# Moving key searches, context work and modulation rows inside a fused PEER and scan kernel

## The chip, the core and the metric

The kernel runs on one core of a Trainium2 chip. The metric is the device time of one launch in microseconds, the median of several executions. The engines are named as in the profile: PE (TensorE, matrix products), DVE (VectorE), ACT (ScalarE), POOL (GpSimd) and SP (SyncE, which only issues transfers here). Each engine, and the list of transfers of SP and of POOL, executes its own program strictly in order.

## What is computed

Two transformer-like blocks on 256 tokens of width 1024, in float32. The first block is a normalisation, one wide projection, an attention that selects keys by an index score, a convolution branch, and then PEER: each token picks 16 of 16384 experts in each of 8 heads and gathers their rows. The second block normalises with shifts and scales that come from `c` (the modulation rows), runs a context of 256 other tokens through a gated linear recurrence (RWKV) in both directions, runs the tokens through the same recurrence from the states so won, and ends with a convolutional feed-forward part.

```python
def peer(h, w_query, sub_keys, expert_u, expert_v):
    q = (h @ w_query).reshape(B, S, 8, 2, 128)
    sc = einsum("bshcd,hckd->bshck", q, sub_keys)   # key scores: 2 x 128 per head and token
    sv, si = top_k(sc, 16)                          # the search
    cand_s = sv[..., 0, :, None] + sv[..., 1, None, :]
    top_s, top_j = top_k(cand_s, 16); eidx = ...    # 16 experts of 16384
    gate = softmax(top_s)
    u = expert_u[eidx]; v = expert_v[eidx]          # gathered rows, 1024 each
    return sum(gelu(u . h) * gate * v)

mod = silu(c) @ ada_w + ada_b                       # modulation rows, for the tokens
cmod = silu(c_ctx) @ ada_w + ada_b                  # and for the context
```

## The kernel before

Line numbers are those of the profile of the kernel before; where the changed kernel's order is shown, they are 3 higher for the searches, the attention and the experts, and 16 to 19 higher from line 950 on.

The 256 tokens are two tiles of 128. The program is written in Python over a framework that gives every instruction a priority by the place where the code issues it, plays the program through a model of the engines, and from that fixes one order for each engine; `tc.issue_after(i)` keeps what stands under it behind instruction `i`. So the order in which code is written sets who goes first, and after that the chip only waits, it does not reorder.

- **0 to 291 us.** The first block up to its residual: index scores (`index(t)`, L629, products L637), gated linear units, queries, keys, values, gates, attention (`attention(t)`, L664: logits L675 and L676, softmax on DVE and ACT, transposes L691, value products L695), the convolution (L762, mean L767), and six modulation rows. A modulation row (`ada_row`, L391) loads 2 MB, multiplies it on DVE by columns of `silu(c)` (L407, 7 instructions of 128x512 for each of its one or two vectors), and has PE sum over the partitions (L412). Rows 0 to 3 are made for the tokens and for the context (n = 2), rows 4 and 5 for the tokens alone; all six are written behind the convolution.
- **291 to 1160 us.** The experts: 16 units, a unit being one head of one tile, first the 8 of tile 0. A unit (`experts`, L865) gathers 16 times 1 MB with an indirect transfer (L875, 9 buffers `G`), forms each gather's scalar products with the tokens on DVE (L880, the dots), and for groups of four the gelu (L886 to L892) and the sum with V, even members on PE (L903, L905) and odd ones on DVE (L909). At the end of a tile the PE sum is added (L896).
- Before a head's unit its keys must be known: `subkeys(h)` (L458) makes the query and the scores of both tiles on PE, `best(t, h, sc)` (L476) searches 16 of 128 twice on DVE (L483 to L487), and `pairs`, `route` and `weigh` pick the 16 experts. `AHEAD` makes heads 1 to 7 within units 1 to 4 of tile 0, and there each head's `best` runs for tile 0 and, behind the unit, also for tile 1. For tile 1 only `pairs`, `route` and `weigh` are left, three units ahead (`LEAD`).
- In the same stretch the engines do other work between the dots: the context's part (its scans, L1006 to L1260), `front(0)` (the second block's first products on tile 0) and `scans0` (the local part of tile 0's scans, both directions d = 0, 1, at the end of which d = 1's MN, RQ and Y are stored). In the code they stand behind all 16 units, so they have the lower priority, and fill what the units leave.
- **1160 to 1591 us.** `front(1)` (from L322), the scans of tile 1 and their combination with tile 0's, modulation rows 6 to 11, the output product and the feed-forward part. SP's loads for it begin with `yy<-Y` (L1526: tile 0's scan outputs, into the buffer that `h` of tile 1 leaves) and the weights.

PSUM banks are handed out by `bank(tag)`: `"ac0"` and `"ac1"` name one bank each, `"ac"` takes them in turn.

Of the kernel before, what the change touches and what calls it, by code (L numbers as in the profile page):

```python
# [25 lines left out]
F32 = mybir.dt.float32  # L26
# [3 lines left out]
AF = mybir.ActivationFunctionType  # L30
# [62 lines left out]
def block_kernel(ctx: ExitStack, tc: tile.TileContext, I, out):  # L93
# [363 lines left out]

    def subkeys(h):  # L458
# [8 lines left out]
        sc = {t: pa.tile([128, 256], F32, tag="sc", name="sc", bufs=6) for t in range(NT)}  # L467
        for t in range(NT):
# [4 lines left out]
            nc.scalar.activation(sc[t], p[:, :256], AF.Copy)  # L473
        return sc
# [71 lines left out]
    with ExitStack() as st:  # L546
# [82 lines left out]
        def index(t):  # L629
# [3 lines left out]
            for g in range(2):  # L633
                for s in range(2):
                    p = bank("ac0")
# [28 lines left out]
        def attention(t):  # L664
# [4 lines left out]
            for g in range(2):  # L669
                for s in range(2):  # L670
                    p = bank("ac0")
# [15 lines left out]
            po = bank("ac0")  # L687
# [24 lines left out]
        for t in range(NT):  # L712
            index(t)

# [13 lines left out]
        sc2 = scv.rearrange("p k s -> p (k s)")  # L728
        nc.scalar.activation(sc2, V("c"), AF.Sigmoid)
        nc.vector.tensor_tensor(sc2, sc2, V("c"), op=OP.mult)  # L730
# [12 lines left out]
        pada = pool("pada", stack=st)  # L743
# [20 lines left out]
        run(chain(*[ada_row(pada, j, 2) for j in range(4)]))  # L764
# [21 lines left out]
        run(chain(*[ada_row(pada, j, 1) for j in range(4, 6)]))  # L786
# [130 lines left out]
    for t in range(NT):  # L917
        if t == 1:
            h2[1] = ph.tile([128, D], F32, tag="h2", name="h2")
            nc.sync.dma_start(out=h2[1], in_=h2d)  # L920
        pacc = [bank("ac", 2) for _ in range(2)]
        for h in range(H):
            if t == 0:
                for g in AHEAD.get(h, ()):
                    with after(*ends, first_gather[0]):
                        sc[g] = subkeys(g)
                    best(0, g, sc[g][0])
                    weigh(0, g, *route(0, g, *pairs(0, g, nc.gpsimd)))
            else:
                for g in range(h + 1 if h else 0, min(h + 2, H)):  # L930
                    with tc.issue_after(unit_end[H + g - LEAD]):
                        weigh(1, g, *route(1, g, *pairs(1, g, nc.gpsimd)))
            unit_end.append(experts(t, h, pacc))
            if t == 0:
                if h == 0:
                    sc01 = pe.tile([128, 256], F32, tag="sc0", name="sc01")
                    subkeys_one(1, sc01)
                    best(1, 0, sc01)
                for g in AHEAD.get(h, ()):
                    best(1, g, sc[g][1])  # L940
# [884 lines left out]
```

## Time and profile before

| | us |
|---|---|
| median of three runs | 1593.75 (1590.28 to 1598.25) |
| the profiled execution | 1593.02 |
| its span in the trace | 1591.3 |
| first gather issued | 291.3 |
| last dots end | 1158.2 |
| VectorE busy in all | 1139.2 |

The trace shows one execution. A row of a group of instructions names the engine, the line, the tile written, the tiles read and a shape; "idle before" is time in which the engine had nothing to do ahead of these instructions, with what ended it. Of TensorE's clock 1.00 is 2.4 GHz and 0.50 is 1.2 GHz.

### The profile page before, as it was taken

How to read it: one execution, taken by the hardware profiler on the slowest of the kernel's cores; microseconds unless marked ns; L12 is line 12 of the kernel's file. 1: busy time of each engine (PE TensorE's matmuls, PEld its weight loads, DVE VectorE, ACT ScalarE, POOL GpSimd, SP SyncE). 2: the span in 40 equal slices, each digit the busy share in tenths (PEclk: the TensorE clock that was granted, in tenths of full speed). 3: DMA queues.
4: the chain of work that ended last, by engine and by line, in shares of the span. 5: the costliest groups of instructions: out<-in, count | busy, mean ns of one | idle time of the engine just before them, and what ended most of it. 6: DMA issues, size and time to landing. Idle time of an engine off the chain costs nothing. (4 is left out here: it accounts for less than half of the span.)

```text
span 1591.3 us, 26450 instructions
## 1 busy us (share of the span) xinstructions
PE 1363.7 (86%) x10140; PEld 889.3 (56%) x10140; DVE 1139.2 (72%) x2495; ACT 516.4 (32%) x1290; POOL 600.4 (38%) x599
## 2 busy tenths in 40 slices
PE   7999979888878888887884979988679898599997
PEld 5744554666435554545432335645344577399997
DVE  3991573699969888989665687787842966456676
ACT  3122230332243333333233242233232223244543
POOL 0000001245555655565542564254500211356663
PEclk9999959999988888878897989879889889799999
DMA  9545463698898999896997999979987541446561
GB/s 352 187 146 167 137 213 111 254 351 329 322 388 304 392 370 368 329 351 266 416 416 308 398 402 357 362 276 380 408 315 274 178 142 57 170 132 188 181 189 53
DMA packets 90197, 435.12 MB, mean 273 GB/s; under 512 B 9996, under 2 KB 14620, under 8 KB 57304
## 3 DMA queue, kind: packets, MB, share of 16 engines
q0 software_dynamic: 36864, 268.45, 42.8%
q1 hardware_dynamic: 52488, 163.67, 30.0%
q8 instruction: 80, 1.31, 0.3%
q10 hardware_dynamic: 720, 1.31, 0.2%
q14 instruction: 45, 0.37, 0.1%
HBM read 428.39 MB, written 5.01 MB: 272 GB/s over the span
## 5 line engine op out<-in xcount | busy, mean ns | idle before, releaser
L875 POOL DMA_INDIRECT G<-in_experts,eidx x256 | 335.2, 1309 | 356.9 <-DVE x L909 229.3
L880 DVE SCALAR_TENSOR_TENSOR G<-G,h 128x1024 f32<-128x1024 f32 x256 | 322.7, 1272 | 18.4 <-DMA G<-in_experts,eidx 14.9
L905 PE MATMUL ac<-G,dg 128*128 128x512 f32 x504 | 280.3, 705 | 51.4 <-ACT dg L903 51.1
L905 PEld LDWEIGHTS ac<-G,dg 128*128 128x128 f32 x504 | 108.6, 226 | 189.1 <-issue 115.0
L909 DVE SCALAR_TENSOR_TENSOR x<-G,ga,x 128x1024 f32<-128x1024 f32 (+1 forms) x131 | 169.8, 1297 | 1.9
L889 ACT ACTIVATE gd<-dots,gate 128x1 f32<-128x1 f32 x256 | 74.0, 290 | 276.9 <-DVE G L880 271.8
L200 POOL TENSOR_TENSOR wl<-wr,wh 128x1024 fp32r<-128x1024 f32 x50 | 122.4, 2463 | 109.5 <-ACT wh L198 105.8
L211 PE MATMUL mm<-wr,big 128*128 128x512 f32 (+1 forms) x352 | 146.6, 570 | 0.0
L211 PEld LDWEIGHTS mm<-wr,big 128*128 128x128 f32 x352 | 64.2, 192 | 71.8 <-issue 69.7
L407 DVE SCALAR_TENSOR_TENSOR acc<-wada,scv,acc 128x512 f32<-128x512 f32 x112 | 82.9, 770 | 28.9 <-DMA wada<-in_ada 21.7
L211 PE MATMUL mm<-bigl,wh 128*128 128x256 f32 x352 | 99.5, 283 | 1.1 <-DVE bigl L345 1.1
L211 PE MATMUL mm<-bigh,wh 128*128 128x256 f32 x352 | 99.6, 284 | 0.4 <-DVE bigh L344 0.4
L211 PE MATMUL mm<-bigh,wl 128*128 128x256 f32 x352 | 99.1, 283 | 0.0
L799 POOL TENSOR_TENSOR sgt<-sgt 128x512 f32<-128x512 f32 x4 | 5.0, 1271 | 242.4 <-DVE sgt L798 242.4
L1638 DVE SCALAR_TENSOR_TENSOR facc<-mm,vec,facc 128x189 f32<-128x189 f32 (+2 forms) x176 | 75.4, 430 | 25.1 <-ACT facc L1631 20.8
L198 ACT ACTIVATE wh<-wr 128x1024 fp32r<-128x1024 f32 x66 | 69.6, 1059 | 71.8 <-PE tp L211 25.4
L211 PEld LDWEIGHTS mm<-bigl,wh 128*128 128x128 f32 x352 | 67.3, 191 | 1.9 <-DVE bigl L345 1.4
L211 PEld LDWEIGHTS mm<-bigh,wh 128*128 128x128 f32 x352 | 67.5, 192 | 1.4 <-DVE bigh L344 0.6
L211 PEld LDWEIGHTS mm<-bigh,wl 128*128 128x128 f32 x352 | 67.2, 191 | 0.4
L211 PE MATMUL mm<-wr,Xh 128*128 128x512 f32 x144 | 66.2, 609 | 0.0
L903 ACT ACTIVATE dg<-ident,ga 128x128 f32<-128x128 f32 x126 | 44.0, 393 | 28.6 <-DVE ga L892 23.3
L762 DVE SCALAR_TENSOR_TENSOR yc<-u,vec,yc 128x256 f32<-128x256 f32 x120 | 52.3, 475 | 0.3
(481 smaller groups left out, 2688.5 us busy)
## 6 DMA issues: line engine op xcount, KB each, us to landing
wr<-in_w_in SPq DMA_DIRECT2D x56, 512.0 KB
wada<-in_ada SPq DMA_DIRECT2D x48, 512.0 KB
wr<-in_ffn_up SPq DMA_DIRECT2D x44, 512.0 KB
wr<-in_ffn_down SPq DMA_DIRECT2D x22, 512.0 KB
wr<-in_w_att SPq DMA_DIRECT2D x16, 512.0 KB
wr<-in_w_gates SPq DMA_DIRECT2D x16, 512.0 KB
wr<-in_w_ple_gate SPq DMA_DIRECT2D x16, 512.0 KB
wr<-in_w_peer_q SPq DMA_DIRECT2D x14, 512.0 KB
```

What stands on the lines that cost most here:

```text
L198: nc.scalar.activation(wh[:, :n], w[:, :n], AF.Copy)
L200: e.tensor_tensor(wl[:, :n], w[:, :n], wh[:, :n].bitcast(F32), op=OP.subtract)
L211: nc.tensor.matmul(o, a, b, start=start and i == 0, stop=stop and i == len(l) - 1)
L407: nc.vector.scalar_tensor_tensor(acc[i], wv, c, acc[i], op0=OP.mult, op1=OP.add)
L762: nc.vector.scalar_tensor_tensor(yc[:, j], u[:, j, k:k + 256], cw[:, j, k:k + 1], yc[:, j], op0=OP.mult, op1=OP.add)
L875: ins = nc.gpsimd.indirect_dma_start(out=b, out_offset=None, in_=I["experts"], in_offset=bass.IndirectOffsetOnAxis(ap=eidx[t, h][:, n:n + ...
L880: nc.vector.scalar_tensor_tensor(b[:, :D], b[:, :D], 1.0, h2[t], op0=OP.mult, op1=OP.mult, accum_out=dots[:, n - g:n - g + 1])
L889: nc.scalar.activation(dg_[:, n:n + 1], dots[:, n:n + 1], AF.Copy, scale=gate[t, h][:, g + n:g + n + 1])
L903: nc.scalar.activation(dg, ident, AF.Copy, scale=c)
L905: nc.tensor.matmul(pacc[q], dg, v[:, q * 512:(q + 1) * 512], start=first and n == to_pe[0], stop=h == H - 1 and n == TOPK - 4)
L909: end = nc.vector.scalar_tensor_tensor(x[:, t, q], v[:, q], c, x[:, t, q], op0=OP.mult, op1=OP.add).ins
L1638: nc.vector.scalar_tensor_tensor(o, pg_[:, a0 + dy:a1 + dy, b0 + dx:b1 + dx], fw[:, j, k_:k_ + 1], o, op0=OP.mult, op1=OP.add)
```

## The change

Three things are edited.

1. `subkeys(h)` stores the second tile's scores in DRAM (`SC_d`, 128 KB a head, for heads 1 to 7). The searches of tile 1 for these heads are no longer made behind the units of tile 0: with `route` and `weigh`, in the units of tile 1, the scores are loaded into one buffer `sc1` and searched.
2. The units become a generator, and the other work is issued between them: five units, the context's part, three units, `front(0)`, one unit, `scans0`, the last seven units.
3. Modulation rows 0 to 3 (and `silu(c)`) are issued right behind `index`, ahead of the gated linear units, and their banks, those of rows 4 and 5, of the index and of the attention are taken in turn from `ac0` and `ac1` instead of one fixed bank.

```diff
+    SC_d = {h: dr.tile([128, 256], F32, name=f"SC{h}") for h in range(1, H)}
     def subkeys(h):
-        sc = {t: pa.tile([128, 256], F32, tag="sc", name="sc", bufs=6) for t in range(NT)}
+        sc = {t: pa.tile([128, 256], F32, tag="sc", name="sc", bufs=4) for t in range(NT)}
...
+        nc.sync.dma_start(out=SC_d[h], in_=sc[1])
         return sc
...
             for g in range(2):
                 for s in range(2):
-                    p = bank("ac0")
+                    p = bank("ac")
...
         for t in range(NT):
             index(t)
+        sc2 = scv.rearrange("p k s -> p (k s)")
+        nc.scalar.activation(sc2, V("c"), AF.Sigmoid)
+        nc.vector.tensor_tensor(sc2, sc2, V("c"), op=OP.mult)
+        pada = pool("pada", stack=st)
+        run(chain(*[ada_row(pada, j, 2, tag="ac") for j in range(4)]))
...
-        run(chain(*[ada_row(pada, j, 2) for j in range(4)]))
...
-    for t in range(NT):
...
+    def in_units():
+        for t in range(NT):
...
                 else:
                     for g in range(h + 1 if h else 0, min(h + 2, H)):
                         with tc.issue_after(unit_end[H + g - LEAD]):
+                            if g:
+                                sc1 = pg.tile([128, 256], F32, tag="sc1", name="sc1")
+                                nc.sync.dma_start(out=sc1, in_=SC_d[g])
+                                best(1, g, sc1)
                             weigh(1, g, *route(1, g, *pairs(1, g, nc.gpsimd)))
                 unit_end.append(experts(t, h, pacc))
...
-                for g in AHEAD.get(h, ()):
-                    best(1, g, sc[g][1])
+                yield
+    units = in_units()
+    def go_on(n):
+        for _ in range(n):
+            next(units, None)
+    go_on(5)
     sA.close()
...
+    go_on(H - 5)
     with ExitStack() as st:
         pq = pool("pq0", stack=st)
         w0 = pool("w0", stack=st)
         rest, *feats = front(0, pq, lambda: use_stage(w0, 8))
+    go_on(1)
     use_stage(w2, W2R)
     scans0(rest, *feats)
+    go_on(H)
```

**Order on PE, end of the first stage.** Before, the products of modulation row 0 (L412, bank `ac_1101`) stand behind the attention's first transposes and value products (L691, L695):

```order
L211 MATMUL mm<-wr,big 128x512 x12
L691 MATMUL tp<-ident,lg 128x128 x2
L211 MATMUL mm<-wr,big 128x512 x10
L695 MATMUL ac_668<-vt,pT 128x64 x2
L691 MATMUL tp<-ident,lg 128x128 x2
L211 MATMUL mm<-wr,big 128x512 x5
L412 MATMUL ac_1101<-cst,acc 128x1 x5
```

Now all four rows' products stand among the large products; here are the second and third of them (`ac_451`, `ac_488`), the head transposes (L603) and the first logits (L678, L679):

```order
L412 MATMUL ac_451<-cst,acc 128x1 x7
L603 MATMUL tp<-ident,qn 128x128 x3
L211 MATMUL mm<-wr,big 128x512 x28
L412 MATMUL ac_488<-cst,acc 128x1 x8
L211 MATMUL mm<-wr,big 128x512 x10
L678 MATMUL ac_787<-bias,flip 128x128
L679 MATMUL ac_787<-kT,qT 128x128
```

The rows moved ahead, and the logits of tile 0, which share the two banks with them, moved behind the third row.

**Order on DVE, searches for tile 1.** Before, in a first unit of tile 0, the search of head 1 for tile 1 (scores `sc_1831`) stands between the dots (L880) and the routing of tile 0 (L519 to L539):

```order
L487 TENSOR_SCALAR si_95<-iu_1937 128x16
L484 MAX_INDEX iu_2119<-sv_94,sc_1831 128x8
L484 MAX_INDEX iu_2126<-sv_94,sc_1831 128x8
L486 MATCH_REPLACE sc_1831<-sv_94,sc_1831 128x128
L880 SCALAR_TENSOR_TENSOR G_1699,dots_1692<-G_1699,h2_1570 128x1024
L519 MAX ts_1961<-cs_1944 128x8
L486 MATCH_REPLACE sc_1831<-sv_94,sc_1831 128x128
L483 MAX sv_94<-sc_1831 128x8
L520 MAX_INDEX tj_1962<-ts_1961,cs_1944 128x8
```

Now such a search (head 2's, scores `sc1_7570`, loaded from DRAM) stands in a unit of tile 1, beside steps of the context's scans (L1201, L1240):

```order
L1201 TENSOR_TENSOR X_4287<-mm_4657,sg_4622 128x4x64 x2
L912 SCALAR_TENSOR_TENSOR x_66<-G_5685,ga_5688,x_66 128x1024
L486 MAX sv_94<-sc1_7570 128x8 x2
L487 MAX_INDEX iu_7572<-sv_94,sc1_7570 128x8
L487 MAX_INDEX iu_7579<-sv_94,sc1_7570 128x8
L1240 TENSOR_TENSOR qw_4668<-mm_4671,dW_4669 128x4x64
L489 MATCH_REPLACE sc1_7570<-sv_94,sc1_7570 128x128 x2
```

Seven searches left the first units of tile 0. They stand now behind the dots of about gathers 113, 128, 145, 161, 177, 193 and 209 of 256. The other work stands later among the gathers than before, by 8 to 16 of them: the products of `front(0)`, which began behind the V sums of gather 142, begin behind those of gather 158.

**Order on DVE and SP, end of the experts.** Before, nothing but the experts' own steps stands around the last dots on DVE (L880, the 256th):

```order
L896 TENSOR_TENSOR x<-ac_3492,x 128x512
L896 TENSOR_TENSOR x<-ac_3493,x 128x512
L887 SCALAR_TENSOR_TENSOR ga<-ga,dots 128x1
L880 SCALAR_TENSOR_TENSOR G,dots<-G,h_3490 128x1024
L892 SCALAR_TENSOR_TENSOR ga<-gb,gd 128x1
L909 SCALAR_TENSOR_TENSOR x<-G,ga,x 128x1024
```

Now the end of `scans0` stands there (LT, AkT, X, RQ, qw; the dots are L883, the V sums L899 and L912):

```order
L883 SCALAR_TENSOR_TENSOR G,dots<-G,h_5936 128x1024
L1143 SCALAR_TENSOR_TENSOR LT<-mm,cmask 128x256
L1145 TENSOR_TENSOR AkT<-mm,cmask 128x256
L1201 TENSOR_TENSOR X<-mm,sg 128x4x64 x2
L1212 TENSOR_TENSOR RQ<-mm,rT 64x4x64 x4
L1240 TENSOR_TENSOR qw<-mm,dW 128x4x64 x2
L890 SCALAR_TENSOR_TENSOR ga<-ga,dots 128x1
L895 SCALAR_TENSOR_TENSOR ga<-gb,gd 128x1
L899 TENSOR_TENSOR x<-ac_5938,x 128x512
L899 TENSOR_TENSOR x<-ac_5939,x 128x512
L912 SCALAR_TENSOR_TENSOR x<-G,ga,x 128x1024
L912 SCALAR_TENSOR_TENSOR x<-G,ga,x 128x512 x2
```

On PE it is alike: the products of that scan (the last 48 of them make MN) stand ahead of the last six V products (L908), behind which `front(1)` begins; before, the last scan product stood ahead of the last ten. On SP, before, the two loads of tile 0's scan outputs (`yy<-Y`) stand apart:

```order
L1526 DMA yy<-Y_7194 128x512
L194 DMA wr<-in_w_ple_gate 128x1024 x4
L194 DMA wr<-in_w_lora 128x1024 x2
L194 DMA wr<-in_w_in 128x1024 x2
L1509 DMA uT<-U_7192 128x4x128
L1510 DMA cbT<-CB_7193 128x4x128
L1016 DMA hat<-in_lora_up 65x512 x4
L1526 DMA yy<-Y_7195 128x512
```

Now they stand together:

```order
L1545 DMA yy<-Y_5275 128x512
L1545 DMA yy<-Y_5276 128x512
L194 DMA wr<-in_w_ple_gate 128x1024 x4
L194 DMA wr<-in_w_lora 128x1024 x2
L194 DMA wr<-in_w_in 128x1024 x2
```

The load of the output of d = 1 moved ahead of the weights. Earlier on SP, the loads of `sc1` for heads 3, 4 and 5 stand one behind another ahead of the last weights of `front(0)`'s first product.

## Rows read from the trace of the kernel before

**Rows 1.** The page: busy time by engine, and three costly groups.

```profile
PE 1363.7 (86%) x10140; PEld 889.3 (56%) x10140; DVE 1139.2 (72%) x2495; ACT 516.4 (32%) x1290; POOL 600.4 (38%) x599
...
L875 POOL DMA_INDIRECT G<-in_experts,eidx x256 | 335.2, 1309 | 356.9 <-DVE x L909 229.3
...
L909 DVE SCALAR_TENSOR_TENSOR x<-G,ga,x 128x1024 f32<-128x1024 f32 (+1 forms) x131 | 169.8, 1297 | 1.9
...
L407 DVE SCALAR_TENSOR_TENSOR acc<-wada,scv,acc 128x512 f32<-128x512 f32 x112 | 82.9, 770 | 28.9 <-DMA wada<-in_ada 21.7
```

**Rows 2.** Windows: busy us of each engine, TensorE clock, DMA share, GB/s.

```profile
280.00:1160.00 880.00, 721.33 (x5729) 431.78 (x5727) 723.25 (x1622) 285.08 (x865) 445.28 (x514) 0.87 0.89 350
320.00:440.00 120.00, 105.64 (x382) 68.96 (x381) 117.77 (x459) 33.85 (x113) 64.41 (x155) 0.93 0.87 332
```

**Rows 3.** Windows, the gathers (L875) alone.

```profile
320.00:440.00 120.00, 33.97 (x29) 0.93 0.87 332
440.00:1160.00 720.00, 290.94 (x219) 0.86 0.91 358
```

**Rows 4.** VectorE by line, 300 to 480: count, busy, mean ns, idle.

```profile
L484 DVE FIND_INDEX8 iu<-sv,sc 128x8 uint32<-128x128 f32 x60 | 16.5, 280 | 0.0
L483 DVE MAX8 sv<-sc 128x8 f32<-128x128 f32 x60 | 14.5, 277 | 0.0
L486 DVE MATCH_REPLACE8 sc<-sv,sc 128x128 f32<-128x128 f32 x30 | 8.1, 272 | 0.0
...
L487 DVE TENSOR_SCALAR si<-iu 128x16 f32<-128x16 uint32 x30 | 4.7, 172 | 0.0
L484 DVE MATCH_VALUE_LOAD iu<-sv,sc 128x8 f32 x60 | 4.4, 74 | 0.0
...
L486 DVE MATCH_VALUE_LOAD sc<-sv,sc 128x8 f32 x30 | 2.2, 75 | 0.0
```

**Rows 5.** Windows of the first stage's end.

```profile
120.00:160.00 40.00, 40.00 (x110) 19.17 (x109) 5.89 (x10) 8.27 (x22) 0.00 (x0) 1.00 0.54 168
160.00:200.00 40.00, 37.54 (x146) 21.71 (x145) 21.48 (x35) 12.73 (x22) 0.00 (x0) 1.00 0.44 132
200.00:240.00 40.00, 30.51 (x105) 22.28 (x105) 27.39 (x44) 12.11 (x32) 0.00 (x0) 0.53 0.65 219
```

**Rows 6.** Timeline of TensorE: start us, duration us, instruction, idle before it.

```profile
227.51 3.81 PE L412 MATMUL ac<-cst,acc 128*128 128x1 f32 x16 [1.42 <-DVE acc L407]
...
232.97 3.78 PE L211 MATMUL mm<-wr,aT 128*128 128x512 f32 x4 [0.69 <-ACT aT L251]
```

**Rows 7.** Windows: two stretches of the second tile's units.

```profile
640.00:760.00 120.00, 96.38 (x1172) 63.10 (x1170) 109.19 (x210) 39.73 (x128) 73.03 (x89) 0.83 0.81 318
760.00:960.00 200.00, 149.86 (x623) 73.90 (x621) 139.47 (x270) 66.57 (x184) 96.35 (x108) 0.85 0.96 389
```

**Rows 8.** Timeline of VectorE at the end of the experts.

```profile
1157.01 1.22 DVE L880 SCALAR_TENSOR_TENSOR G<-G,h 128x1024 f32<-128x1024 f32 x1
...
1160.16 1.42 DVE L909 SCALAR_TENSOR_TENSOR x<-G,ga,x 128x512 f32<-128x512 f32 x2
```

**Rows 9.** Timeline of TensorE there.

```profile
1148.24 7.65 PE L905 MATMUL ac<-G,dg 128*128 128x512 f32 x12 [5.09 <-ACT dg L903]
1160.97 1.97 PE L322 MATMUL tp<-ident,x 128*128 128x128 f32 x8 [5.08 <-DVE x L909]
```

**Rows 10.** Timeline of SyncE's DMA queue there.

```profile
1158.26 0.32 SPq L1526 DMA_DIRECT2D yy<-Y  x1
1158.68 1.79 SPq L194 DMA_DIRECT2D wr<-in_w_ple_gate  x4
```

**Rows 11.** Timeline of VectorE in the second tile's scans: the same steps.

```profile
1307.94 0.41 DVE L1127 SCALAR_TENSOR_TENSOR LT<-mm,cmask 128x256 f32<-128x256 f32 x1
...
1312.36 0.77 DVE L1196 TENSOR_TENSOR RQ<-mm,rT 64x256 f32<-64x256 f32 x2 [0.53 <-PE mm L1193]
...
1321.54 0.43 DVE L1224 TENSOR_TENSOR qw<-mm,dW 128x256 f32<-128x256 f32 x1 [1.20 <-PE mm L1223]
```

More of the change, by code (lines that the diff above doesn't have):

```diff
@@ L670, in attention @@
                 for s in range(2):
-                    p = bank("ac0")
+                    p = bank("ac")
                     for b in range(2):
@@ L686, in attention @@
             nc.vector.reciprocal(se, se)
-            po = bank("ac0")
+            po = bank("ac")
             for h in range(H):
@@ L741, in block_kernel @@
              lambda t, p: nc.scalar.activation(vt[:, t], p, AF.Copy))
-        pada = pool("pada", stack=st)
         for t in range(NT):
@@ L785, in block_kernel @@
         cT = yc,
-        run(chain(*[ada_row(pada, j, 1) for j in range(4, 6)]))
+        run(chain(*[ada_row(pada, j, 1, tag="ac") for j in range(4, 6)]))
         mix = sgt[:, :, :D]
@@ L916, in block_kernel @@
     unit_end = []
-    for t in range(NT):
[L918 to L923, printed above, removed]
-                for g in AHEAD.get(h, ()):
[L925 to L939, printed above, removed]
-                    best(1, g, sc[g][1])
+    def in_units():
+        for t in range(NT):
+            if t == 1:
+                h2[1] = ph.tile([128, D], F32, tag="h2", name="h2")
+                nc.sync.dma_start(out=h2[1], in_=h2d)
+            pacc = [bank("ac", 2) for _ in range(2)]
+            for h in range(H):
+                if t == 0:
+                    for g in AHEAD.get(h, ()):
+                        with after(*ends, first_gather[0]):
+                            sc[g] = subkeys(g)
+                        best(0, g, sc[g][0])
+                        weigh(0, g, *route(0, g, *pairs(0, g, nc.gpsimd)))
+                else:
+                    for g in range(h + 1 if h else 0, min(h + 2, H)):
+                        with tc.issue_after(unit_end[H + g - LEAD]):
+                            if g:
+                                sc1 = pg.tile([128, 256], F32, tag="sc1", name="sc1")
+                                nc.sync.dma_start(out=sc1, in_=SC_d[g])
+                                best(1, g, sc1)
+                            weigh(1, g, *route(1, g, *pairs(1, g, nc.gpsimd)))
+                unit_end.append(experts(t, h, pacc))
+                if t == 0:
+                    if h == 0:
+                        sc01 = pe.tile([128, 256], F32, tag="sc0", name="sc01")
+                        subkeys_one(1, sc01)
+                        best(1, 0, sc01)
+                yield
```

3 lines of the change are left out of this document (removed).

## The prediction

> **What bounds the kernel now.** I read the page first, then the windows of the experts, then the ends of the first two stages line by line. On the page no engine is full: VectorE is busy 72% of the span, and POOL's gathers wait 229.3 us for a V sum on VectorE, that is for a free buffer [rows 1]. An average hides the stages, so the windows come next. Of the experts' 880 us VectorE is busy 723 and the DMA engines are at 0.89 [rows 2]; but from 320 to 440 us, where the heads are made, VectorE has 117.8 of 120 us and carries 29 gathers, one per 4.1 us, while the some 219 after it take 3.3 us each [rows 3]. So there are three places to judge: the ramp, bound by VectorE; the rest of the gathers, where VectorE waits now and then in its program for other work; and the two joints, the first gather and the end of the experts, where things are serial. After the experts nothing is edited.
>
> **Modulation rows earlier.** Between 120 and 160 us VectorE does 5.9 us of work, and in the 40 us from 200 on 27.4, while TensorE drops to 30.5 busy at a granted clock of 0.53, nearly all of it at the lower level of 1.2 GHz [rows 5]. Late in that stretch TensorE waits 1.42 us for a row's accumulation, spends 3.81 us on its sums, and only then goes on to the attention's output product at 232.97 [rows 6]. With rows 0 to 3 gone, that chain of 5.2 us leaves the path, and so does the VectorE time of three rows (row 0 is already half early), 3 x 14 x 0.77 us = 32 us by the mean of L407 [rows 1], which stands among the attention's steps. What is late next is the attention itself: in the new order tile 0's logits are behind the third row's sums because they share two banks, so its softmax comes later and moves from beside the large products towards the tail. That gives part back. Least gain: a loss of 3, if tile 0's later softmax meets tile 1's. Most: TensorE's 9.5 idle us in the last window plus the 5.2, so 15. I take 10, in the upper half, because one row alone gives 5.2.
>
> **Searches out of the ramp.** The searches of 15 heads (one tile each) cost 16.5 + 14.5 + 8.1 + 4.7 + 4.4 + 2.2 = 50.4 us [rows 4], 3.36 us each; seven leave, 23.5 us. VectorE is busy 98% there, so at most about 23 come back. What is late next is DMA: its share is 0.87 of 120 us [rows 2], 104 us of transfers, and the seven stores add 0.9 MB, some 2 us at 350 GB/s. That leaves 13 to 14 us by the share; by the rate of the DMA-bound windows of tile 1 (389 GB/s at 0.96 [rows 7]) the 39.8 MB moved take 102 us, 18 less. I take 16, with 8 and 23 as ends.
>
> **Searches into tile 1.** Seven times 3.36 us come back. The first three fall where VectorE has 109.2 of 120 us (640 to 760 us before), so they cost 0.91 x 10.1 = 9 us; the other four where it has 139.5 of 200 and DMA is at 0.96 [rows 7], so DMA is the cover and they cost nothing. Without that cover it is 23.5 us. A loaded search waits for SP, but the load stands far ahead: each loads when the search before it frees the one buffer, one unit earlier (some 50 us). I take +9, from 0 to 23.5.
>
> **The other work at the end of the experts.** Before, the 256th dots end at 1158.23 and x is complete 3.35 us later, at 1161.58 [rows 8]; TensorE had done its last V products at 1155.9 and waited 5.08 us for x [rows 9]. In the new order the end of `scans0` stands behind the last dots on VectorE, its products on TensorE ahead of the last six V products, and the V sums behind both. What this chain takes is seen in tile 1's scans: from LT at 1307.94 to the end of RQ at 1313.13 is 5.2 us, and qw came at 1321.54 with the other direction's work between [rows 11]. For the 48 products of MN I take 3 us, since the chain ahead of them, of steps that wait for each other, takes 5.2; the 8.4 us from RQ's end to qw are the upper end. Then the six V products, 12 records in 7.65 us [rows 9], then two additions of half rows, a V sum of 1.3 [rows 1] and the last two of 1.42 [rows 8], about 4. Together 5.2 + 3 + 7.7 + 4 = 20 us against 3.35: 16.5 us later. Against it, what stands behind the dots no longer stands ahead of them: some 5 us of VectorE's steps (LT 0.41, a pair of RQ 0.77, qw 0.43 [rows 11]) and a part of the waits for TensorE in them. I take off 7.5, so +9; ends +4 and +21.
>
> **The round trip through DRAM and SP.** Fourteen transfers of 128 KB are 1.8 MB, 5 us at 350 GB/s; as DMA binds only parts of the stage I take +1 (0 to +8). The upper end holds two waits on SP: `front(0)`'s weights stand behind the load for head 5, which waits for head 4's search, and behind the experts four weights stand behind both loads of scan outputs. Before, the first load was released by the last dots, at 1158.26, and the weights followed at 1158.68 [rows 10]; now they follow the store of d = 1's output, but x is later by as much.
>
> **The sum**, against the profiled execution of 1593.0 us (1.7 us of it outside the span): -10 - 16 + 9 + 9 + 1 = -7, so 1586. That execution is 0.7 us under the median of 1593.75, so the forecast in the median's terms is 1586.7; I give 1587. About 0.5%, 8 us, is what a measurement can tell from no change here.
>
> **Rivals.**
> - *The stage is elastic (1566, chance 0.20).* The searches hide wholly (0 instead of +9), the ramp gives its 23 and the scan's end hides behind the last groups (+4): -10 - 23 + 0 + 4 + 1 = -28, so 1565 to 1566. For it speaks that VectorE idles 157 us of the stage [rows 2]; against it that these waits lie in the order of the program and are not free to be filled, and that the first half of the new place is nearly as full as the old one [rows 7]. The Trainium skill, in Perfetto Trace Analysis, section Optimization Strategy, says that where the most contended engine changes over time, interleaving the regimes may help, which is what moving searches from the ramp into tile 1 does; by that rule, with the two costs ahead left out, the sum would be -10 - 16 = -26, 1567.
> - *The end of the experts decides (1609, chance 0.24).* One mechanism: on VectorE and TensorE the end of the scan stands between the last dots and x, at +20 with the MN products near their upper end and little taken off before the dots; the searches cost 14, the ramp gives only its 13 and the first stage 6: -6 - 13 + 14 + 20 + 1 = +16, and 1609. It decides as soon as the chain behind the last dots exceeds what the joint and the ramp give and the searches leave, 5 us in this sum and 17 in mine. For it speaks that all of it is serial; against it that the chain's steps are short.
> - *DMA sets the whole stage (1593, chance 0.06).* Then moving VectorE's work gives nothing in the ramp or costs nothing in tile 1, and only the joints count: -10 + 9 + 1 = 0. For it speaks the share of 0.96 in rows 7, against it 0.87 in the ramp and 0.81 from 640 to 760. The Trainium skill, in DMA: Bandwidth & Descriptors, section Where 436 GB/s comes from, puts the limit of reads from memory at some 358 GB/s for a core; by that estimate the experts' 308 MB would need 861 of their 880 us. The 200 us at 389 GB/s [rows 7] are above it, so here the measurement decides and I keep the chance low.
> - *The searches don't leave the ramp* is excluded: the new order shows them behind gathers 113 to 209.
>
> **How the numbers follow.** The forecast, with the terms between their ends (1575 to 1598), has 0.50; its middle lies 1 us above 1585.8, the bound of faster by over 0.5%, so I count 0.24 of it as faster and 0.26 as within. Elastic, 0.20, is faster; the end, 0.24, slower; DMA, 0.06, the same. Faster 0.44, same 0.32, slower 0.24. The likeliest case's own range is 1575 to 1598; the range that leaves out 2 in 10 reaches from the elastic case to near that of the end: 1564 to 1606.
>
> **What would show it.** The first gather some 10 us earlier than 291.3, TensorE's sums of rows 0 to 3 below 200 us; from the 11th to the 39th gather 3.5 us each instead of 4.1; the seven searches with the dots of tile 1 around them and VectorE's windows there at 36 or more of 40; between the last dots and `front(1)`'s first transpose some 20 us with LT, X, RQ and qw in them; from there on 430 us as before. The forecast is wrong if the first gather doesn't come earlier, if tile 1's gathers slow by over 0.1 us each (that is 13 us), or if x is complete within 8 us of the last dots.

## The result, and the profile after the change

The changed kernel takes 1612.83 us (median of 4 runs, 1610.29 to 1615.04) against 1592.87 for the kernel before in the same measurement: ratio 1.0121, 95% interval 1.0100 to 1.0142. It is slower by 1.2%, where 1587 was forecast with a range up to 1606. Its profiled span is 1611.1 us, 19.8 longer than the 1591.3 of before.

The timelines of both, read at the same events, say where the 19.8 us are (us; `front1` is `front(1)`'s first transpose, which needs the complete x; the last dots are those of the 256th gather):

| stretch | before | after | difference | forecast |
|---|---|---|---|---|
| start to first gather | 291.3 | 285.7 | -5.7 | -10 |
| first gather to the 40th | 151.5 | 146.7 | -4.8 | -16 |
| the 40th to the last gather | 699.6 | 705.5 | +5.9 | +9 and +1 |
| last gather to the end of the last dots | 15.7 | 16.1 | +0.4 | -7.5 |
| last dots to `front1` | 2.8 | 22.4 | +19.6 | +16.5 |
| `front1` to the end | 430.3 | 434.7 | +4.4 | 0 |

`front1` of the changed kernel, answering to [rows 9]:

```profile
1176.41 1.97 PE L322 MATMUL tp<-ident,x 128*128 128x128 f32 x8 [2.89 <-DVE x L912]
```

The page answers to [rows 1]: busy time by engine, then the gathers, the V sums and the row sums.

```profile
PE 1358.1 (84%) x10140; PEld 885.2 (55%) x10140; DVE 1142.5 (71%) x2495; ACT 514.4 (32%) x1290; POOL 593.0 (37%) x599
...
L878 POOL DMA_INDIRECT G<-in_experts,eidx x256 | 324.5, 1267 | 363.2 <-DVE x L912 225.8
...
L912 DVE SCALAR_TENSOR_TENSOR x<-G,ga,x 128x1024 f32<-128x1024 f32 (+1 forms) x131 | 167.7, 1280 | 1.8
...
L407 DVE SCALAR_TENSOR_TENSOR acc<-wada,scv,acc 128x512 f32<-128x512 f32 x112 | 83.5, 762 | 21.5 <-DMA wada<-in_ada 18.8
```

The work of each engine is what it was (VectorE 1142.5 us against 1139.2): nothing became dearer, it stands elsewhere. The windows say where, as [rows 2, 5, 7] did: busy us of PE, PEld, DVE, ACT, POOL, then TensorE's granted clock, DMA share, GB/s.

```profile
120.00:160.00 40.00, 40.00 (x111) 19.15 (x110) 28.64 (x53) 4.49 (x7) 0.00 (x0) 1.00 0.78 252
160.00:200.00 40.00, 36.90 (x136) 21.45 (x134) 18.03 (x30) 16.07 (x37) 0.00 (x0) 0.91 0.48 155
200.00:240.00 40.00, 33.55 (x113) 21.59 (x113) 11.97 (x19) 9.62 (x28) 0.00 (x0) 0.70 0.38 132
...
320.00:440.00 120.00, 95.92 (x348) 62.79 (x347) 102.47 (x315) 34.73 (x115) 67.15 (x135) 0.91 0.87 344
...
640.00:760.00 120.00, 91.02 (x890) 56.07 (x890) 109.57 (x227) 38.20 (x115) 65.93 (x78) 0.76 0.78 302
760.00:960.00 200.00, 146.63 (x862) 76.92 (x858) 144.56 (x341) 60.72 (x184) 91.35 (x119) 0.87 0.96 386
```

The row sums did move (VectorE 28.64 us at 120 to 160 instead of 5.89). The ramp is the surprise: VectorE fell from 117.8 to 102.5 us of 120, so it has room now, and yet the same windows for the gathers alone show 30 of them instead of the 29 of [rows 3].

```profile
320.00:440.00 120.00, 34.47 (x30) 0.91 0.87 344
440.00:1160.00 720.00, 274.94 (x215) 0.85 0.90 354
```

The end of the experts looks as the prediction drew it. VectorE's timeline (start, duration, instruction, idle before it and who ended that), answering to [rows 8]:

```profile
1152.77 1.22 DVE L883 SCALAR_TENSOR_TENSOR G<-G,h 128x1024 f32<-128x1024 f32 x1
1153.91 0.08 DVE L883 DVE_READ_ACCUMULATOR G<-G,h 128x1 f32 x1
1153.91 0.42 DVE L1143 SCALAR_TENSOR_TENSOR LT<-mm,cmask 128x256 f32<-128x256 f32 x1
...
1157.54 0.77 DVE L1212 TENSOR_TENSOR RQ<-mm,rT 64x256 f32<-64x256 f32 x2 [1.45 <-PE mm L1209]
1160.45 0.42 DVE L1240 TENSOR_TENSOR qw<-mm,dW 128x256 f32<-128x256 f32 x1 [2.14 <-PE mm L1239]
1168.04 0.42 DVE L1240 TENSOR_TENSOR qw<-mm,dW 128x256 f32<-128x256 f32 x1 [7.16 <-POOL dW L1229]
...
1171.85 0.69 DVE L899 TENSOR_TENSOR x<-ac,x 128x512 f32<-128x512 f32 x1 [1.31 <-PE ac L908]
1173.55 0.69 DVE L899 TENSOR_TENSOR x<-ac,x 128x512 f32<-128x512 f32 x1 [1.01 <-PE ac L908]
1174.28 2.73 DVE L912 SCALAR_TENSOR_TENSOR x<-G,ga,x 128x1024 f32<-128x1024 f32 x3
```

From LT to the first qw it is 7 us (8.2 forecast), but then the second qw waits 7.16 us for a product on POOL. POOL's timeline shows why:

```profile
1166.17 1.26 POOL L1546 TENSOR_TENSOR yy<-yy 128x512 f32<-128x512 f32 x1 [27.11 <-DMA yy<-Y]
1167.39 0.61 POOL L1229 TENSOR_TENSOR dW<-cst,wC 128x256 f32<-128x256 f32 x1
```

The sum of the two scan outputs stands ahead of the second dW, and its operand goes through DRAM. Last, SyncE's queue from 677 to 847 us; a row with x3 and 110.73 us is three loads, the first issued at 723.60 and the last ending at 834.33:

```profile
677.93 0.35 SPq L940 DMA_DIRECT2D sc<-SC  x1
...
723.60 110.73 SPq L940 DMA_DIRECT2D sc<-SC  x3
834.43 2.92 SPq L194 DMA_DIRECT2D wr<-in_w_ple_gate  x5
```

`front(0)`'s weights follow 0.1 us behind the third load. Before, they were issued at 780.80:

```profile
780.80 8.70 SPq L194 DMA_DIRECT2D wr<-in_w_ple_gate  x4
```

### The profile page after: what moved, and what is told of

The parts are those of the page before. It is cut to its first block, busy times and chain, and to the rows that moved or that the text cites. A ratio compares the mean times of both kernels' runs of the same rounds, so it can differ in the third digit from the quotient of the medians.

```text
span 1611.1 us, 26474 instructions
## 1 busy us (share of the span) xinstructions
PE 1358.1 (84%) x10140; PEld 885.2 (55%) x10140; DVE 1142.5 (71%) x2495; ACT 514.4 (32%) x1290; POOL 593.0 (37%) x599
## 5 line engine op out<-in xcount | busy, mean ns | idle before, releaser
L878 POOL DMA_INDIRECT G<-in_experts,eidx x256 | 324.5, 1267 | 363.2 <-DVE x L912 225.8
L883 DVE SCALAR_TENSOR_TENSOR G<-G,h 128x1024 f32<-128x1024 f32 x256 | 322.0, 1268 | 33.9 <-DMA G<-in_experts,eidx 30.6
L908 PE MATMUL ac<-G,dg 128*128 128x512 f32 x504 | 281.3, 705 | 74.8 <-ACT dg L906 74.8
L908 PEld LDWEIGHTS ac<-G,dg 128*128 128x128 f32 x504 | 107.6, 225 | 211.0 <-issue 109.9
L912 DVE SCALAR_TENSOR_TENSOR x<-G,ga,x 128x1024 f32<-128x1024 f32 (+1 forms) x131 | 167.7, 1280 | 1.8
L211 PE MATMUL mm<-h2T,wr 128*128 128x256 f32 x224 | 50.8, 379 | 0.0
```

Of the source, the lines that this page charges most:

```text
L211: nc.tensor.matmul(o, a, b, start=start and i == 0, stop=stop and i == len(l) - 1)
L878: ins = nc.gpsimd.indirect_dma_start(out=b, out_offset=None, in_=I["experts"], in_offset=bass.IndirectOffsetOnAxis(ap=eidx[t, h][:, n:n + ...
L883: nc.vector.scalar_tensor_tensor(b[:, :D], b[:, :D], 1.0, h2[t], op0=OP.mult, op1=OP.mult, accum_out=dots[:, n - g:n - g + 1])
L908: nc.tensor.matmul(pacc[q], dg, v[:, q * 512:(q + 1) * 512], start=first and n == to_pe[0], stop=h == H - 1 and n == TOPK - 4)
L912: end = nc.vector.scalar_tensor_tensor(x[:, t, q], v[:, q], c, x[:, t, q], op0=OP.mult, op1=OP.add).ins
```

## The experiments

Ratios are to the kernel before, run on the same chip beside each group, with the 95% interval.

**The three edits apart.** e1 is the DRAM edit alone (stores, loads and the search in tile 1), e2 the generator with context, `front(0)` and `scans0` between heads, e3 the rows with the shared banks, e5 is e2 and e3.

```diff
+         nc.sync.dma_start(out=SC_d[h], in_=sc[1])                  (e1)
+                             nc.sync.dma_start(out=sc1, in_=SC_d[g])
+                             best(1, g, sc1)
-                 for g in AHEAD.get(h, ()):
-                     best(1, g, sc[g][1])
+    go_on(5) ... go_on(H - 5) ... go_on(1) ... go_on(H)             (e2)
+         run(chain(*[ada_row(pada, j, 2, tag="ac") for j in range(4)]))   (e3)
```

> Only the searches through DRAM (edit 1), order of the code and modulation rows as before. Theory: this edit alone pushes the scan's end behind the last dots (in this kernel's order both last MN steps stand behind all 256 dots, before behind 244 and 247), because with the searches gone the gathers run ahead of the other work in the scheduler's model. So ramp -5 us, searches in tile 1 +7, end +20: about 1615, and 18 to 24 us from the last dots to x. Rival (the interleaving of units makes the end late): ramp -5, searches +7, end as before: 1593 to 1597.

> Only the interleaving of the other work with the units (edit 2). Theory: its order has the last MN steps behind 242 and 244 dots, so the end stays at 3 to 4 us and the time at 1593, within 4 us. Rival (the interleaving makes the end late): 1605 to 1615.

> Only the modulation rows earlier (edit 3). Theory: first gather 5 to 6 us earlier, as in the changed kernel; the last MN steps stand behind 253 and 256 dots, so a part of the late end is here too, +5 to +12: 1592 to 1600. Rival (the first stage is all that this edit touches): 1587 to 1588.

> Edits 2 and 3 without the searches through DRAM. Theory: first gather 5 to 6 us earlier, ramp as before, last MN steps behind 242 and 243 dots, so x is complete 3 to 5 us behind the last dots: 1586 to 1589, faster than before. Rival (the late end comes from the interleaving): 1605 to 1613.

Measured: e1 1.0116 (1.0069 to 1.0162), e2 1.0006 (0.9984 to 1.0028), e3 1.0075 (1.0051 to 1.0099), e5 0.9983 (0.9961 to 1.0005). The DRAM edit, with the order that comes with it, carries the loss, alone and on top of the others. And the parts don't add: e3 alone costs 12 us, yet with e2 beside it nothing. e3 touches only the first stage, which it shortens by nothing in its profile (first gather at 291.6); but the framework fixes the whole order anew, and in e3's the late scan's last products stand behind 253 and all 256 dots (before: 244 and 247), and `front1` comes at 1171.95. An edit moves what it doesn't touch, and without any load the order alone sets e3 and e5 0.9% apart.

**SyncE's queue.** The waits of SyncE's queue, 440 to 1180 us, in e1 (line waited for: us, times, longest):

```profile
SPq L937 <- DVE si L490: 119.0, 5, 57.3
...
SPq L937 <- DVE iu L487: 62.4, 1, 62.4
```

A load stands there until the search before it lets the one buffer go, and all later loads of SyncE behind it. e1_b3 gives e1 three buffers; r3 gives them to the changed kernel, r2 puts its stores on ScalarE's queue, r4 does both.

```diff
-        nc.sync.dma_start(out=SC_d[h], in_=sc[1])                    (r2, r4)
+        nc.scalar.dma_start(out=SC_d[h], in_=sc[1])
-  sc1 = pg.tile([128, 256], F32, tag="sc1", name="sc1")              (e1_b3, r3, r4)
+  sc1 = pg.tile([128, 256], F32, tag="sc1", name="sc1", bufs=3)
```

> Only the searches through DRAM, with three buffers for the loaded scores instead of one. In the run with one buffer, SyncE waited 49 us for searches ahead of front(0)'s weights, TensorE 6.7 us for a weight, and between 880 and 900 us hardly anything ran. Theory (the single buffer in SyncE's row costs in tile 1): the stall at the weights goes, gathers 168 to 208 take 150 us instead of 171, time 1592 to 1600. Rival (the late scan end costs in this kernel too): 1605 or more.

> The changed kernel with the seven stores of the scores issued by ScalarE instead of SyncE; the order on VectorE at the end of the experts is the same as in the changed kernel. Theory: on SyncE each store waits for its head's scores, and the context's first weights stand behind them (402 us for the last five, before 376 on); the context's chain starts later by this and everything that hangs on it, up to x. Without it the context's first MN step comes at 538 to 546 us instead of 551, front(1) at 1163 to 1171 instead of 1176: 1599 to 1607. Rival (VectorE's order, with the context behind gather 40, sets its start): 549 to 553 and 1609 to 1614.

> The changed kernel with three buffers for the loaded scores. Theory (as in the run with edit 1 alone, where this gave 14 us): SyncE no longer waits for searches ahead of front(0)'s weights, front(0)'s gate comes earlier than 901 us by 5 to 15, time 1597 to 1606. Rival (here the context's late start sets it, the weights come in time): 1608 to 1614.

> Both: stores on ScalarE and three buffers. If the two waits on SyncE are the cause, they add up: front(1) at 1155 to 1163, 1590 to 1599. If the end of the scans behind the last dots is a cause of its own (it stands there in this order too, behind 255 and 256 dots), the gap stays 15 us or more and the time over 1603.

Measured: e1_b3 1.0016 (0.9998 to 1.0034), 14 us better than e1; r2 1.0128 (1.0089 to 1.0167) and r3 1.0102 (1.0062 to 1.0143), neither told from the change; r4 1.0060 (1.0041 to 1.0079), 8 us of the 20 back. So three buffers, with the new order of all engines that comes with them, take back nearly all of e1's loss, but not the whole change's. The theory that the length of the queue's waits explains it all fell here. e1_b3's loads still wait 136.8 us in 4 waits, against 181.4 in e1,

```profile
SPq L937 <- DVE si L490: 136.8, 4, 63.8
```

and is as fast as before. Nor is it the place of `front(0)`'s weights alone. In e1_b3 they are issued at 813 us, 6 us sooner than in e1 and 33 later than before; in x1 (below) at 799, as early as in c1 and d3 (below), which lose nothing. SyncE's queue in e1_b3, then TensorE's wait for these weights in the changed kernel and before, 440 to 1180 us:

```profile
813.39 6.97 SPq L194 DMA_DIRECT2D wr<-in_w_ple_gate  x4
...
PE mm L211 <- DMA wr<-in_w_ple_gate: 2.8, 1, 2.8
...
PE mm L211 <- DMA wr<-in_w_ple_gate: 0.8, 1, 0.8
```

**The end of the experts.** r1 moves the loads and the sum of the scan outputs behind the last head, y_dve puts that sum on VectorE, x1 takes tile 0's candidate sums from POOL to VectorE, which also changes the order.

```diff
+    with tc.issue_after(unit_end[-1]):                               (r1)
-    nc.gpsimd.tensor_tensor(ys[0], ys[0], ys[1], op=OP.add)          (y_dve)
+    nc.vector.tensor_tensor(ys[0], ys[0], ys[1], op=OP.add)
-  weigh(0, g, *route(0, g, *pairs(0, g, nc.gpsimd)))                 (x1)
+  weigh(0, g, *route(0, g, *pairs(0, g, nc.vector)))
```

> The changed kernel, with the two loads of tile 0's scan outputs and their addition on POOL put behind the end of the experts. Theory: in the changed kernel the addition stood on POOL ahead of the second dW and waited for the store and load of d = 1's output through DRAM; dW released qw, and ACT's dg for the last V sums stood behind qw. Without it the wait of 7.2 us of VectorE for POOL's dW goes: gap from the last dots to front(1) 15 to 17 us instead of 22.4, time 1605 to 1607. Rival (the chain of the scan itself takes the time): the gap stays at 20 or more and the time at 1611 to 1613.

> The changed kernel with the addition of the two scan outputs on VectorE instead of POOL, so that POOL's products for the late scan no longer stand behind a load from DRAM. If VectorE's wait of 7.2 us for them is on the path, the gap behind the last dots falls from 22 us to about 15 and the time to 1603 to 1607. If TensorE or the other work sets the joint, the wait turns into another and the time stays at 1610 to 1614.

> The changed kernel with the pair sums of tile 0's heads 1 to 7 on VectorE instead of POOL (98 small additions of some 0.1 us each, about 10 us of VectorE in the ramp). Theory for the ramp: after the searches had left it, heads waited for POOL, whose pair sums stand behind gathers that wait for a buffer; without that wait gathers 0 to 39 take 135 to 143 us instead of 146.7 although VectorE has more to do. Rival (VectorE or DMA still binds the ramp): 147 to 155 us. In this order the last MN steps stand behind 245 and 246 dots, so the gap at the end should be 3 to 5 us in either case: 1588 to 1600.

Measured: r1 1.0131 (1.0094 to 1.0169). Its edit left the order of VectorE, ScalarE, POOL and SyncE as it was, so it tells nothing of the end. It is a second execution of the changed kernel's order, though, and shows how far two traces of one order differ: its `front1` comes 7 us sooner.

```profile
1169.41 1.97 PE L322 MATMUL tp<-ident,x 128*128 128x128 f32 x8 [2.89 <-DVE x L912]
```

In y_dve, 1.0106 (1.0085 to 1.0128), the wait for POOL is gone, and in its place VectorE itself waits for the load:

```profile
1163.85 0.42 DVE L1240 TENSOR_TENSOR qw<-mm,dW 128x256 f32<-128x256 f32 x1 [1.79 <-PE mm L1239]
1169.57 0.69 DVE L1546 TENSOR_TENSOR yy<-yy 128x512 f32<-128x512 f32 x1 [5.30 <-DMA yy<-Y]
1170.18 0.42 DVE L1240 TENSOR_TENSOR qw<-mm,dW 128x256 f32<-128x256 f32 x1
```

The gap stays at 20.6 us: the store and load through DRAM are on the path, whichever engine adds. x1 is the telling one, 1.0097 (1.0066 to 1.0129): its order ends the late scan behind 245 and 246 dots, the gap is 2.7 us as before, and still `front1` comes at 1177.8, as late as in the changed kernel. VectorE's last dots in x1 and TensorE's `front1`:

```profile
1173.82 1.22 DVE L883 SCALAR_TENSOR_TENSOR G<-G,h 128x1024 f32<-128x1024 f32 x1
...
1177.78 1.97 PE L322 MATMUL tp<-ident,x 128*128 128x128 f32 x8 [4.67 <-DVE x L912]
```

The gap closed and its time stood ahead of it. x1 has another order on every engine and 98 more steps on VectorE, so it doesn't show that the changed kernel's gap costs nothing; it shows that as much is lost without a late end.

**The other work earlier.** s_22 hands out the heads as 5, 2, 2 instead of 5, 3, 1, so that `front(0)` and `scans0` come sooner (in it `front(0)` takes tile 0 before its last head is added). g8 has 8 gather buffers instead of 9; with them the other work stands among the dots where it stood before.

```diff
-    go_on(H - 5)                                                     (s_22)
+    go_on(2)
-    go_on(1)
+    go_on(2)
-                b = pG.tile([128, 2 * D], F32, tag="G", name="G", bufs=9)   (g8)
+                b = pG.tile([128, 2 * D], F32, tag="G", name="G", bufs=8)
```

> The changed kernel with the other work one unit earlier: five units, the context's part, two units, front(0), two units, scans0, the rest; the last MN steps then stand behind 198 and 199 dots instead of 256. Theory (the end of the experts is what made the change slower): gap of 3 to 4 us, last dots as late as 1154 or up to 8 us later since the steps lie ahead of them again: 1592 to 1600. Rival (the loss is spread over tile 1's units and the end only shows it): the last dots end 15 us or more later and the time stays over 1605.

> The changed kernel with 8 gather buffers instead of 9. With them the other work stands where it stood before the change: context's first MN products behind 66 dots, the late scan's behind 238. If that place decides, the gap between the last dots and front(1) falls from 22 us to under 4, front(1) begins at 1145 to 1156, and the time is 1588 to 1598. If the searches' price in tile 1 decides, the time stays at 1610 or more, with the gathers slower by what a buffer less costs.

Measured: s_22 1.0293 (1.0268 to 1.0318), g8 1.0178 (1.0156 to 1.0200), both with a gap of 2.7 us. The other work comes early and the gathers pay: in g8 the last one is issued at 1182.96 instead of 1137.9. POOL's waits, 440 to 1200 us, of g8 and then of the changed kernel:

```profile
POOL G L878 <- DVE x L912: 254.1, 68, 19.1
```

```profile
POOL G L878 <- DVE x L912: 208.8, 69, 24.1
```

45 us more waiting for a free buffer. So putting the other work earlier doesn't bring the time back; g8 changes a buffer too and doesn't clear that place wholly.

**The searches, the loads and the place, one by one.** d3 is e5 with the searches of heads 5 to 7 moved into tile 1 and their scores kept on the chip: no transfer. c1 is the changed kernel without the seven searches and loads; its tile 1 gathers tile 0's experts, as many. c2 has the searches and loads with c1's experts, c3 the loads and one step per search.

```diff
+        sc = {t: pg.tile([128, 256], F32, tag="sk1", name="sk1", bufs=3) if t and h >= 5   (d3)
+              else pa.tile([128, 256], F32, tag="sc", name="sc", bufs=4) for t in range(NT)}
...
+                            if g >= 5:
+                                best(1, g, sc[g][1])
-  sc1 = ...; nc.sync.dma_start(out=sc1, in_=SC_d[g]); best(1, g, sc1)       (c1)
-  weigh(1, g, *route(1, g, *pairs(1, g, nc.gpsimd)))                        (c1, c2, c3)
+  weigh(1, g, *route(1, g, *pairs(1 if g == 0 else 0, g, nc.gpsimd)))
-                                best(1, g, sc1)                             (c3)
+                                nc.vector.max(out=sv[:, 1, g, 0, :8], in_=sc1)
```

> The two edits without the DRAM edit (1592.0 us, first transpose of front(1) at 1148.7), with the searches of heads 5 to 7 of tile 1 moved into tile 1, their scores kept in on-chip memory: no store, no load. In the new order the first of context's MN products stands behind 71 dots instead of 64, the end of the late scan behind all 256 instead of 242. If the transfers and SyncE's queue are what costs, 1588 to 1594. If the place of the searches, or the other work's place in the order, is what costs, front(1) begins at 1156 to 1166 and the time is 1597 to 1604.

> The changed kernel without tile 1's searches and loads for heads 1 to 7; tile 1 takes tile 0's candidates there, so it gathers other experts, as many. The stores stay. If the searches' time in tile 1 is what costs (7 x 3.36 us on VectorE, the price that the ramp doesn't give back), front(1) begins 18 to 24 us earlier, near 1155, and the time is 1588 to 1594. If the other work's later place is what costs (in this order still 73 to 75 dots for context, 251 for the late scan), little comes back: 1603 to 1611.

> The changed kernel with all its searches and loads; only the candidates that tile 1 uses for heads 1 to 7 are tile 0's, so that it gathers the same experts as c1. If c1's 23 us come from the searches and loads, this one stands at 1607 to 1616; if they come from the experts that are gathered, it stands at 1588 to 1595.

> As c2, with the loads kept and one step of VectorE (the first maximum, read from the loaded scores) in place of each of the seven searches. If the 3.36 us of VectorE for each search make the cost, 1588 to 1596 and a gap under 6 us behind the last dots; if the loads behind SyncE's waits make it, 1604 to 1613; half of each gives 1597 to 1603.

Measured, as a ladder: e5 0.9983 (0.9961 to 1.0005), c1 0.9980 (0.9962 to 0.9997), c3 1.0113 (1.0065 to 1.0160), c2 1.0131 (1.0089 to 1.0172), the whole change 1.0121. Each step changes one thing, and the order with it. From e5 to c1 seven searches leave the ramp for nothing, 23.5 us of VectorE by [rows 4], the stores come in, and the time doesn't move: the ramp's gain is nought by the end. From c1 to c3 the loads come in, 0.9 MB and seven steps of 0.42 us, and 21 us are lost (0.0133 of 1594). From c3 to c2 the rest of the searches comes in and costs 0.0018, 3 us, inside intervals of some 7 us to either side. c2 clears the changed experts. d3, three searches without transfers, is at 1.0005 (0.9986 to 1.0024), 0.0022 above e5: not told from it.

c1 by itself reads as if the searches made the loss; c3 shows that it isn't so. The waits of SyncE's queue in c3, 440 to 1180 us, hold the loads, and there are no loads in c1; c1's queue waits too, though, and longer for the buffers of the weights (166.9 us against 102.0):

```profile
SPq L1032 <- PE mm L975: 177.7, 7, 64.2
SPq L940 <- DVE ts L522: 144.8, 4, 54.9
...
SPq L194 <- PE mm L211: 102.0, 19, 19.3
```

In c1:

```profile
SPq L194 <- PE mm L211: 166.9, 29, 48.7
```

What VectorE did in 440 to 1120 us, in c3 and then in c1:

```profile
440.00:1120.00 680.00, 537.91 (x4723) 312.25 (x4722) 535.00 (x979) 219.89 (x654) 343.86 (x331) 0.85 0.90 352
```

```profile
440.00:1120.00 680.00, 547.04 (x4989) 323.68 (x4987) 548.63 (x1006) 232.20 (x683) 346.07 (x343) 0.87 0.93 368
```

With the loads there VectorE does 13.6 us less in the same time, TensorE 9.1 less, and DMA moves 352 GB/s instead of 368: everything waits a little more.

What stays open is by which path. That the loads wait for their buffer is shown; that this waiting makes the loss is not. The loads also enter the plan from which the order of all engines is fixed: c1's order differs from c3's on every engine, and e1's from e1_b3's, so the 14 us of the three buffers are the buffers and a new order together. In c3 the 208th gather is 12 us later than in c1 and `front1` 29.5 (in c3, then in c1): more than half of the loss falls behind 1000 us, where no load is left (the last is issued at 963).

```profile
1182.14 1.97 PE L322 MATMUL tp<-ident,x 128*128 128x128 f32 x8 [4.48 <-DVE x L912]
...
1152.61 1.97 PE L322 MATMUL tp<-ident,x 128*128 128x128 f32 x8 [4.67 <-DVE x L912]
```

A kernel with the one order and the other's loads wasn't tried.

**A faster version.** e5's trace shows a wait in the second half, VectorE's `yy` for POOL, which was 3.4 us before:

```profile
DVE yy L1612 <- POOL gg L1588: 11.2, 1, 11.2
```

e7 is e5 with that product on VectorE.

```diff
-        nc.gpsimd.tensor_tensor(gain[t], gain[t], r_lng, op=OP.mult)
+        nc.vector.tensor_tensor(gain[t], gain[t], r_lng, op=OP.mult)
```

> Edits 2 and 3 without the searches through DRAM (1592, front(1) at 1148.7, 12 us earlier than before, but the rest 8.6 us longer, of which VectorE waits 11.2 us for the product gg on POOL behind three weight splits), with the product gg on VectorE. Theory: the wait goes and the 12 us stay: 1579 to 1586, faster than before by 0.5 to 0.9%. Rival (the rest is longer for another reason): 1588 to 1593.

Measured: 1586.42 us, 0.9943 (0.9916 to 0.9971), the one version with the same result that is shown to beat both kernels. Its profile doesn't credit the moved product, though: `front1` to the end takes 438.8 us as in e5 (438.9), and VectorE's new product waits 8.5 us for a row from DMA.

```profile
DVE gg L1588 <- DMA row_lng<-in_rows: 8.5, 1, 8.5
```

The 5.9 us by which its span is shorter (1581.7 against 1587.6) stand ahead of `front1`, in e7 and then in e5:

```profile
1142.88 1.97 PE L322 MATMUL tp<-ident,x 128*128 128x128 f32 x8 [4.48 <-DVE x L909]
...
1148.65 1.97 PE L322 MATMUL tp<-ident,x 128*128 128x128 f32 x8 [4.47 <-DVE x L909]
```

Up to there VectorE, ScalarE, POOL and SyncE have the same order in both, so this is a difference between two executions, no larger than the 7 us of r1. That e7 is faster than e5 isn't shown: their intervals overlap (0.9916 to 0.9971 and 0.9961 to 1.0005).

## Why the prediction was wrong

Two terms carry the miss, the round trip through DRAM and the ramp. Set beside the experiments, each with its order, the forecast reads: edits 2 and 3 give -3 (e5), where the first stage was to give -10; the searches out of the ramp 0 (e5 to c1) for -16; the loads +21 (c1 to c3) for +1; the rest of the searches +3 (c3 to c2) for +9. That makes +21, against 19 measured. The +9 for the late end has no experiment of its own.

- **The mis-sized term is "the round trip through DRAM and SP".** Its mechanism was written down, weights behind a load that waits for a search, and priced at +1 with 0 to +8, on the ground that DMA binds only in parts and that each load stands far ahead. By c1 against c3 the loads, with the order that comes with them, are worth +21. The step that failed is that fourteen transfers of 128 KB were priced by their bytes, and the waits behind them at 8 at most. The mechanism itself is in the trace: five loads of the changed kernel wait 133.8 us for the searches' last step (`si`), and three of them stand ahead of `front(0)`'s weights, which are issued at 834 us where e5, without loads, has them at 778 and c1 at 800. But TensorE waits only 2.8 us for these weights (0.8 before), e1_b3 with them at 813 is as fast as the kernel before, and x1 with them at 799 is not. So how much of the 21 us is the queue and how much the order stays open.
- **The ramp, -16, is -4.8 to the 40th gather and nought by the end.** VectorE's cover was real and went (117.8 to 102.5 of 120), but the gathers did not follow: 30 instead of 29. From the 11th to the 39th they took 4.18 us each, 4.27 before, where 3.5 was forecast. The DMA share, which the sum had as the next bound, stayed at 0.87; what grew is other waits of the same ramp, 320 to 440 us. TensorE waits 23.8 us for ScalarE's `dg` (14.4 before), VectorE 6.6 us for POOL's sums of candidates (1.4 before); the changed kernel, then before:

```profile
PE ac L908 <- ACT dg L906: 23.8, 6, 10.4
...
DVE ts L522 <- POOL cs L510: 6.6, 3, 2.8
...
PE ac L905 <- ACT dg L903: 14.4, 4, 5.1
...
DVE ts L519 <- POOL cs L507: 1.4, 1, 1.4
```

x1 moved those sums; its ramp took 144.1 us, 2.6 less. The step that failed here is that VectorE's 98% and the DMA share behind it were read as the only bounds.
- **The searches in tile 1, +9,** come out at 3 us in c2 against c3 (0.0018) and at 3.5 in d3 for three of them. Both lie inside the intervals; by c2 against c3 neither nought nor +9 is excluded.
- **The late end, +16.5 less 7.5.** The chain itself was sized well, 22.4 us against 20, by another mixture, and so in part by luck: 3.8 us of V products instead of 7.7, since the first four ran during the wait, and 7.2 us for POOL's dW behind the sum that goes through DRAM, which the sum hadn't. The 7.5 taken off didn't come: the last gather to the end of the dots is 16.1 us against 15.7. And x1 and c3 (gaps 2.7 and 2.5, `front1` at 1178 and 1182) are as late without it. The rival "the end of the experts decides" gave 1609 and came nearest. In the timeline its first stage (-6) and its joint (+20) stand as it had them; its -13 for the ramp and +14 for the searches do not, and x1 and c3 speak against the joint as the place where the loss is made.
- **The first stage, -10, gave -5.7,** with TensorE's sums of the first rows at 141 and 162 us as expected. But that is one execution. All sixteen kernels with edit 3 have the same order on VectorE and ScalarE up to the first gather, and in their traces it comes at 285.5 to 293.5 us; in the four without the edit at 290.5 to 292.2. It goes with the granted clock from 200 to 240 us: 0.70 where it came by 286, as in the changed kernel, 0.59 or 0.60 where it came behind 291, as in e3 (291.6) and c1 (293.5). So the edit gives between 6 and -2, and -10 nowhere.
- **Elastic and DMA-bound** are both out. The Trainium skill's advice in Perfetto Trace Analysis, Optimization Strategy, to interleave regimes of different contention gave 1567 by that sum. By c1, emptying the ramp alone brings nothing here. The limit of some 358 GB/s that the Trainium skill has in DMA: Bandwidth & Descriptors, Where 436 GB/s comes from, again doesn't bound it: the trace shows 386 GB/s over 200 us after the change.
- **What would make it wrong** was named as the first gather, 0.1 us more per gather in tile 1, or x within 8 us. None of them happened; gathers 113 to 256 take 3.40 us each against 3.36. What did fail is the ramp's sign, 3.5 us a gather. The list looked at the terms of the sum that were thought large, and had no line for SyncE's queue, which was cheap to watch.

## What to carry to other kernels

Price a small transfer not by its bytes alone: list what is issued behind it on the same engine, and for how long its buffer or operand keeps it there, and then ask which engine waits for that. More buffers, with a new order, brought 14 us in e1; in the changed kernel only buffers and another queue together told, 8 of 20. Where a framework fixes one order for the whole program, an edit's own price can be smaller than the change of order that comes with it (e3: +12 us alone, nothing beside e2), so measure parts and pairs before adding them up. A gap at a joint shows where lateness ends; where it closes without the time moving, look ahead of it. And before a few us of one trace are put down to an edit, look at a second execution of the same order: here it moved `front1` by 7 us and the first gather by up to 8.

## What the runs showed that was not expected

- Freeing 15 of 120 us of VectorE, the engine that was 98% busy, brought one gather more in that stretch.
- The granted clock of TensorE at 200 to 240 us was 0.53 before, 0.59 in e3 and 0.70 after the change, in which VectorE, not TensorE, had the lighter work (11.97 instead of 27.39 us); the level of 2.4 GHz was granted for a larger part of it. With one and the same order of the first stage on VectorE and ScalarE it lay between 0.59 and 0.70 from kernel to kernel.
- One gather buffer of nine, with the order that goes with it, is worth 45 us of POOL's waiting and 0.6% of the time (g8).
